# One product for two in the MLP's up-projection of a split-precision transformer block, with edits at the kernel's start and end

## The chip, the core and the metric

The kernel runs on one core of one Trainium2 chip. The metric is the device time of one execution in microseconds. The time of the kernel before is 2253.19 us, the median of three runs (2246.54 to 2254.56 us).

## What is computed

Two transformer blocks on 256 tokens of width 2048, all in float32. The first block mixes the tokens with a gated delta rule and an RWKV recurrence, attends to 256 memory tokens and ends with an MLP; the second has two kinds of local attention and a layer norm over each token. The part that the change is mostly about is the MLP, and the end of the program is the layer norm:

```python
hn = _rmsnorm(h, norm_mlp[l])                       # 256 x 2048
h = h + jnp.square(jax.nn.relu(hn @ mlp_w_up[l])) @ mlp_w_down[l]   # 2048 x 8192, 8192 x 2048
...
x = _layer_norm(DEEPNORM_ALPHA * x + out, ln_gain[layer], ln_bias[layer])
```

## The kernel before

**Split numbers.** Every large product is made of three. A float32 operand is split in a high part (rounded by ScalarE to the type that TensorE reads fast) and a low part (VectorE subtracts the high part from the number). Of weights W and activations x the kernel adds `hi(W) x hi(x)`, `hi(W) x lo(x)` and `lo(W) x hi(x)` in PSUM. For weights this is done in `piece` (L129 to L142): SyncE loads 256 rows and 512 columns (tile `raw`, 512 KB), `act` at L140 writes `whi`, the subtraction at L141 writes `wlo`. `raw`, `whi` and `wlo` have three buffers each. For activations `split` (L232) does it; the tiles are `ah` and `al`, each of 4 k-tiles of 128 rows and 256 tokens (`act_tiles`, L222, eight buffers in all).

**Two shapes of product.** `ws_parts` (L262) keeps the weights stationary: for each of four blocks `c` of 128 columns and each k-tile it gives TensorE three products with 256 tokens as the moving operand. The sums of two blocks share a PSUM bank (a bank holds 512 float32 columns), so four blocks take two banks. `as_parts` (L286) keeps the activations stationary and moves 512 columns of the weights, again three products for each k-tile and each half `t` of the tokens; `tail` says how many of the last pieces are held back, so that half 0 ends that much before half 1. `mm` (L100) issues all of these, so they all have line L101 in the profile, and `tt`, `stt` and `act` give VectorE's and ScalarE's instructions the lines L107, L116 and L104.

**The MLP** (L1229 to L1275). `mlp_up(b)` computes 2048 of the 8192 inner channels in four calls of `ws` (16 calls in all, 64 blocks of 128 channels, 16 k-tiles each), and `emit` (L1241) turns the sums of each block into its output: ScalarE's Relu from PSUM, VectorE's product of the sums with that, then `split` into `uh` and `ul`. `mlp_down(b)` uses `as_` and adds into `accd`. The order is up(0), up(1), down(0), up(2), down(1), up(3), down(2), down(3). `psum_phase(n)` (L85) divides the 8 PSUM banks: n for tiles of `mmt` (the sums), the rest for `pst`; from L1110 on there are four of each. Ahead of the MLP stand `xattn_wo` (L1218, `as_`) with the transposes of L1219; behind it `rstd` (L1278) and the second block.

**The order of the work.** Each engine has one queue, served in order. The program's order on each queue is laid down at build time by a scheduler that goes by priorities and its own times; only some stretches are ordered by hand (`manual_schedule`: TensorE in the first stage and in the last call of `as_`, SyncE's queue at the start).

**The start** (L151 to L173, L322 to L330): x and the first weights are loaded, x is transposed on TensorE (`tr`, L186) and split, and the 304 small columns of the first projection are computed from them (`ws` at L411).

**The end** (L1452 to L1479). The last product is added to `h`, VectorE takes the statistics, and `layer_norm(t)` normalises half `t` in four parts of 512 columns. Parts 0 to 2 of half 0 and part 0 of half 1 go over ScalarE (scale and shift), then a product with the gain and a sum with the bias, on GpSimd for half 0 (the third part's product on VectorE) and on VectorE for half 1; the other parts take two VectorE instructions each. Every part's output is issued on SyncE's queue.

```python
    for n in range(4):
        s = slice(512 * n, 512 * n + 512)
        if n < 3 - 2 * t:
            act(h[t][:, s], h[t][:, s], AF.Identity, scale=rl, bias=nb_)
```

Of the kernel before, what the change touches and what calls it, by code (L numbers as in the profile page):

```python
# [9 lines left out]
F32 = mybir.dt.float32  # L10
# [10 lines left out]
C_DECAY = 0.5 * math.exp(-0.5)  # L21
INV_LAT = 42.0
PART = 0.66

# [39 lines left out]
def block_kernel(tc, a, out, dbg=None, stop=99):  # L64
# [63 lines left out]

    def piece(W, r0, nk, cols, o=0):  # L129


        n = sum(c[1] for c in cols)
        with tc.high_priority():
            raw = fix.tile([128, nk, n], F32, name="raw", tag="raw", bufs=3)
            for c0, m, d in cols:
                nc.sync.dma_start(out=raw[:, :, d:d + m],
                                  in_=W[r0:r0 + nk * 128, c0:c0 + m].rearrange("(k p) n -> p k n", p=128))
            hi, lo = (fix.tile([128, nk * n + 64], F32R, name=x, tag=x, bufs=3)[:, o:o + nk * n]
                      .rearrange("p (k n) -> p k n", k=nk) for x in ("whi", "wlo"))
            last["act"] = act(hi, raw)  # L140
            last["dve"] = nc.vector.tensor_tensor(out=lo, in0=raw, in1=hi.bitcast(F32), op=SUB)  # L141
        return hi, lo  # L142
# [39 lines left out]
    xinit = cst[:, K_X0:K_X0 + 256]  # L182

    def tr(o, i):
        n = i.shape[0]
        nc.tensor.transpose(o, i, ident[0:n, 0:n])  # L186
# [34 lines left out]

    def act_tiles(where=None, bufs=8):  # L222

        hs, ls = [], []
        for _ in range(bufs // 2):
            h = (where or fix).tile([128, 4, T], F32R, name="ah", tag="act", bufs=bufs)
            l = (where or fix).tile([128, 4, T], F32R, name="al", tag="act", bufs=bufs)
            hs += [h[:, i, :] for i in range(4)]
            ls += [l[:, i, :] for i in range(4)]
        return hs, ls  # L230
# [31 lines left out]
    def ws_parts(W, cols, xh, xl, emit, kts=None, r0=0, needs=(), first=()):  # L262
# [19 lines left out]
        with tc.high_priority():  # L282
            for c in range(n):
                emit(c, acc[c // 2][:, c % 2, :])

    def as_parts(W, c0, xh, xl, emit, kts=None, r0=0, ahead=None, needs=(), tail=1):  # L286
# [682 lines left out]
    def main():  # L969
# [4 lines left out]
        def mem_in(i):  # L974

            q = i // 4
            if i >= 4:
# [3 lines left out]
                if i % 4 == 0:  # L981
                    ht, lt = (fix.tile([128, 4, T], F32R, name=n, tag="act", bufs=8) for n in ("ah", "al"))
                    for n, t_ in (("h", ht), ("l", lt)):
                        mem[n] += [t_[:, k, :] for k in range(4)]
                    with tc.high_priority():
                        rstd_part(lambda t, _: src[:, t, :], mem["ss"], q - 1)
# [228 lines left out]

    hh, hl = act_tiles()
    for n in range(4):
# [9 lines left out]


    rp2 = rstd(by_tok(h), "rmlp")  # L1229
    r2 = fix.tile([128, 2], F32, name="r2")  # L1230
# [4 lines left out]
    def mlp_up(b):  # L1235
        uh, ul = [], []
        for q in range(4):
            u1 = mp.tile([128, 4, T], F32R, name="uh", tag="u", bufs=16)
            u2 = mp.tile([128, 4, T], F32R, name="ul", tag="u", bufs=16)

            def emit(c, p, u1=u1, u2=u2):  # L1241
                r = mp.tile([128, T], F32, name="relu", tag="relu", bufs=2)
                act(r, p, AF.Relu)
                tt(r, p, r, MUL)
                split(r, u1[:, c, :], u2[:, c, :])
            ws(a["mlp_w_up"][0], [(2048 * b + 512 * q, 512, 0)], hh, hl, emit)
            uh += [u1[:, i, :] for i in range(4)]
            ul += [u2[:, i, :] for i in range(4)]
# [4 lines left out]
    def mlp_down(b, u):  # L1253
        for n in range(4):
# [10 lines left out]
            if b == 3:  # L1265
                transposed(by_tok(h), gains["final"], fh, fl, range(4 * n, 4 * n + 4))

# [8 lines left out]


    rf = rstd(by_tok(h), "rf")  # L1278
    sp2, close_s2 = open_pool("blk2")
# [149 lines left out]
    yp, close_y = open_pool("y")  # L1429
    shift(yp, 128)  # L1430
    for more, x in zip(act_tiles(yp, 4), (yh, yl)):
# [19 lines left out]

    def layer_norm(t):  # L1452
        mv = s2([128, 2], "mv", bufs=2)
        nc.vector.bn_aggr(out=mv, in_=st[t])
        rl = s2([128, 1], "rl", bufs=2)
        ts(rl, mv[:, 1:2], 1e-5, ADD)
        powc(rl, rl, mhalf[:, 0:1])
        nb_ = s2([128, 1], "nb_", bufs=2)
        stt(nb_, mv[:, 0:1], -1.0, rl, MUL, MUL)
        for n in range(4):  # L1460
            s = slice(512 * n, 512 * n + 512)
            if n < 3 - 2 * t:
                act(h[t][:, s], h[t][:, s], AF.Identity, scale=rl, bias=nb_)
                tt(h[t][:, s], h[t][:, s], lng[:, s], MUL, eng=nc.gpsimd if t == 0 and n < 2 else None)
                tt(h[t][:, s], h[t][:, s], lnb[:, s], ADD, eng=nc.gpsimd if t == 0 else None)
            else:
                stt(h[t][:, s], h[t][:, s], mv[:, 0:1], lng[:, s], SUB, MUL)
                stt(h[t][:, s], h[t][:, s], rl, lnb[:, s], MUL, ADD)
            nc.sync.dma_start(out=out[0, t * 128:(t + 1) * 128, s], in_=h[t][:, s])

    for n in range(4):
# [6 lines left out]
        with tc.manual_schedule(engines={nc.tensor.engine}) if n == 3 else nullcontext():  # L1478
            as_(a["w_out_2"][0], 512 * n, yh, yl, emit_o, tail=2 if n == 3 else 1)  # L1479
    close_ln()  # L1480
# [28 lines left out]
```

## Time and profile before

| | us |
|---|---|
| three runs, median (lowest to highest) | 2253.19 (2246.54 to 2254.56) |
| the profiled execution | 2262.2 |
| its span, first to last instruction | 2260.5 |
| busy in the span: TensorE products / its weight loads | 2200.2 / 2019.2 |
| VectorE / ScalarE / GpSimd | 1389.2 / 1120.5 / 269.4 |
| mean granted clock of TensorE | 0.986 |

The profile is of one execution; times in it count from the first instruction. TensorE's products overlap, so the time of one product (its row says 0.28 us) is longer than the distance from one start to the next, which is what counts in a dense stretch.

### The profile page before, as it was taken

The numbers are of one execution on the slowest core, as the hardware profiler recorded it, in microseconds if no ns is written. First come the engines' busy times: TensorE is split into PE (matmuls) and PEld (weight loads), VectorE is DVE, ScalarE is ACT, GpSimd is POOL, SyncE is SP. The second block draws the span as 40 slices with busy tenths as digits, with TensorE's granted clock in tenths as the row PEclk, the third lists the DMA queues.
The fourth block names the chain that finished last, engine by engine and source line by source line (L and its number), as shares of the span: only waits on it lengthen the run. The fifth ranks groups of instructions, "written<-read, shape, count | busy, mean of one in ns | idle before, by whom it ended". The sixth has DMA issues, their size and how long they took to land.

```text
span 2260.5 us, 39043 instructions
## 1 busy us (share of the span) xinstructions
PE 2200.2 (97%) x15506; PEld 2019.2 (89%) x15506; DVE 1389.2 (61%) x2236; ACT 1120.5 (50%) x1802; POOL 269.4 (12%) x540
## 2 busy tenths in 40 slices
PE   8999999999999999999999999999999999999996
PEld 8998989788988899889998898899888999888975
DVE  5576676675644555555554455555556676767765
ACT  5455554564444445445454444344344665656542
POOL 0027254165200000000000000000000000011101
PEclk9999999899999999999999999999999999999998
DMA  6654344353466654566666666666656667665654
GB/s 203 186 163 132 96 145 136 97 152 108 148 217 212 188 170 148 157 187 187 188 188 192 194 190 188 195 188 192 192 188 212 192 189 192 179 181 163 176 187 137
DMA packets 229061, 391.77 MB, mean 173 GB/s; under 512 B 39887, under 2 KB 47821, under 8 KB 228494
## 3 DMA queue, kind: packets, MB, share of 16 engines
q1 hardware_dynamic: 227297, 385.63, 56.8%
q10 hardware_dynamic: 1036, 3.58, 0.4%
q8 instruction: 121, 1.98, 0.3%
q14 instruction: 63, 0.51, 0.1%
q0 software_dynamic: 544, 0.07, 0.0%
HBM read 386.25 MB, written 2.97 MB: 172 GB/s over the span
## 4 chain that ended last, share of the span: by engine, by line
PE 87%; DVE 4%; DMA 3%; POOL 3%; ACT 2%; issue 1%; SPq 0%; POOLq 0%; ACTq 0%; DVEq 0%
PE acc L101 79%; POOL Xt L107 1%; DMA raw<-in_w_in_dram 1%; POOL X L107 1%; DVE wlo L141 1%; PE o2p L101 1%; PE s2p L101 1%; DMA nb<-scr 1%; PE t2p L186 1%; PE op L101 1%; PE xs L101 0%; PE xo L101 0%; ACT whi L104 0%; PE tp L186 0%; DMA rT<-in_mem_dram 0%
## 5 line engine op out<-in xcount | busy, mean ns | idle before, releaser
L141 DVE TENSOR_TENSOR wlo<-raw,whi 128x1024 fp32r<-128x1024 f32 (+1 forms) x696 | 853.3, 1227 | 697.7 <-ACT whi L104 692.8
L104 ACT ACTIVATE whi<-raw 128x1024 fp32r<-128x1024 f32 (+1 forms) x696 | 734.9, 1057 | 854.3 <-PE acc L101 734.4
L101 PE MATMUL acc<-ah,whi 128*128 128x256 f32 x3120 | 885.6, 284 | 2.5 <-DVE ey L107 1.8
L101 PE MATMUL acc<-al,whi 128*128 128x256 f32 x3120 | 876.2, 281 | 0.0
L101 PE MATMUL acc<-ah,wlo 128*128 128x256 f32 x3120 | 873.1, 281 | 1.3 <-DVE wlo L141 1.3
L101 PEld LDWEIGHTS acc<-ah,whi 128*128 128x128 f32 x3120 | 589.6, 189 | 8.5 <-issue 3.1
L101 PEld LDWEIGHTS acc<-al,whi 128*128 128x128 f32 x3120 | 589.9, 189 | 1.4 <-issue 0.9
L101 PEld LDWEIGHTS acc<-ah,wlo 128*128 128x128 f32 x3120 | 588.1, 189 | 2.6 <-DVE wlo L141 2.4
L101 PE MATMUL acc<-whi,al 128*128 128x512 f32 x704 | 275.8, 392 | 0.0
L101 PE MATMUL acc<-wlo,ah 128*128 128x512 f32 x704 | 275.7, 392 | 0.0
L101 PE MATMUL acc<-whi,ah 128*128 128x512 f32 x704 | 265.4, 397 | 4.0 <-DVE qky L107 2.6
L101 PE MATMUL acc<-wlo,uh 128*128 128x512 f32 x512 | 199.5, 390 | 0.0
L101 PE MATMUL acc<-whi,ul 128*128 128x512 f32 x512 | 199.2, 389 | 0.0
L101 PE MATMUL acc<-whi,uh 128*128 128x512 f32 x512 | 179.5, 389 | 0.0
L101 PEld LDWEIGHTS acc<-whi,ah 128*128 128x128 f32 x704 | 132.9, 189 | 30.8 <-DVE qky L107 2.8
L101 PEld LDWEIGHTS acc<-whi,al 128*128 128x128 f32 x704 | 133.1, 189 | 27.8
L101 PEld LDWEIGHTS acc<-wlo,ah 128*128 128x128 f32 x704 | 133.3, 189 | 26.6
L101 PEld LDWEIGHTS acc<-whi,ul 128*128 128x128 f32 x512 | 96.1, 188 | 20.0
L101 PEld LDWEIGHTS acc<-whi,uh 128*128 128x128 f32 x512 | 96.1, 188 | 19.8
L101 PEld LDWEIGHTS acc<-wlo,uh 128*128 128x128 f32 x512 | 96.1, 188 | 19.7
L107 POOL TENSOR_TENSOR Xt<-X,nb 128x60 f32<-128x60 f32 (+24 forms) x186 | 80.1, 431 | 162.4 <-DMA nb<-scr 148.6
L1351 POOL MEMSET klz<- 64x256 f32 x8 | 2.5, 307 | 701.5 <-DMA raw<-in_w_in_dram 701.2
(523 smaller groups left out, 1869.3 us busy)
## 6 DMA issues: line engine op xcount, KB each, us to landing
raw<-in_w_in_dram SPq DMA_DIRECT2D x240, 512.0 KB, 3.7
raw<-in_mlp_w_up_dram SPq DMA_DIRECT2D x128, 512.0 KB, 3.7
raw<-in_mlp_w_down_dram SPq DMA_DIRECT2D x128, 512.0 KB, 3.9
raw<-in_w_out_dram SPq DMA_DIRECT2D x64, 512.0 KB, 4.7
raw<-in_xattn_wk_dram SPq DMA_DIRECT2D x32, 512.0 KB, 3.9
raw<-in_xattn_wv_dram SPq DMA_DIRECT2D x32, 512.0 KB, 5.4
raw<-in_xattn_wq_dram SPq DMA_DIRECT2D x32, 512.0 KB, 3.8
raw<-in_xattn_wo_dram SPq DMA_DIRECT2D x32, 512.0 KB, 3.9
```

The costliest lines, as they stand in the source:

```text
L101: nc.tensor.matmul(o, l, r, start=start, stop=stop)
L104: return nc.scalar.activation(o, i, f, **kw)
L107: (eng or nc.vector).tensor_tensor(out=o, in0=x, in1=y, op=op)
L141: last["dve"] = nc.vector.tensor_tensor(out=lo, in0=raw, in1=hi.bitcast(F32), op=SUB)
L186: nc.tensor.transpose(o, i, ident[0:n, 0:n])
L1351: nc.gpsimd.memset(kl[other, e, :].bitcast(F32), 0.0)
```

## The change

- `ws_both` replaces `ws` in `mlp_up`: `hi(W)` meets `hi(x)` and `lo(x)` in one product of 512 columns (the moving operand is two runs of 256 columns, 1024 elements apart), and `lo(W)` meets `hi(x)` in one of 256, which goes to the first half of the bank. Each block of 128 channels has a bank of its own, and `emit` adds the two halves first: one copy on ScalarE and one sum on VectorE more for each block.
- For that, the high and low parts of four k-tiles of x lie in one tile (`act_tiles`, and the same tiles in the first stage); the tag has four buffers of twice the size. The `wlo` tile of `ws_both` is used from element 56 on, the `whi` tile from 0.
- PSUM is divided 7 and 1 for the MLP, and 4 and 4 again behind it; the transposes of the last down-projection take their tiles from the seven.
- Start: eleven products of 512 columns on a tile of zeros, ahead of the rest, into a tile that nothing reads.
- End: all parts but one go over VectorE alone; the last part of half 1 goes over ScalarE and GpSimd and is issued on ScalarE's queue; `tail` is 3, not 2. One placement constant is 160, not 128.

```diff
+WARM = 11
-    def piece(W, r0, nk, cols, o=0):
+    def piece(W, r0, nk, cols, o=0, ol=None):
...
+    idle = xnp.tile([128, 512], F32R, name="idle")
+    nc.vector.memset(idle.bitcast(F32), 0.0)
+    with tc.high_priority():
+        spare = mmt([128, 512], "spare")
+        for i in range(WARM):
+            mm(spare, idle[:, 0:128], idle, start=(i == 0), stop=(i == WARM - 1))
...
-            h = (where or fix).tile([128, 4, T], F32R, name="ah", tag="act", bufs=bufs)
-            l = (where or fix).tile([128, 4, T], F32R, name="al", tag="act", bufs=bufs)
-            hs += [h[:, i, :] for i in range(4)]
-            ls += [l[:, i, :] for i in range(4)]
+            x = (where or fix).tile([128, 2, 4, T], F32R, name="ah", tag="act", bufs=bufs // 2)
+            hs += [x[:, 0, i, :] for i in range(4)]
+            ls += [x[:, 1, i, :] for i in range(4)]
+            if both is not None:
+                both += [x[:, :, i, :] for i in range(4)]
...
+    def ws_both(W, c0, xh, xb, emit):
+        acc = [mmt([128, 2, T], "acc") for _ in range(4)]
+        for i in range(0, 16, 2):
+            hi, lo = piece(W, i * 128, 2, [(c0, 512, 0)], 0, 56)
+            for c in range(4):
+                cc = slice(c * 128, c * 128 + 128)
+                for j in range(2):
+                    k = i + j
+                    mm(acc[c], hi[:, j, cc], xb[k], start=(k == 0), stop=False)
+                    mm(acc[c][:, 0, :], lo[:, j, cc], xh[k], start=False, stop=(k == 15))
+        with tc.high_priority():
+            for c in range(4):
+                emit(c, acc[c])
...
+    psum_phase(7)
     rp2 = rstd(by_tok(h), "rmlp")
...
             def emit(c, p, u1=u1, u2=u2):
                 r = mp.tile([128, T], F32, name="relu", tag="relu", bufs=2)
-                act(r, p, AF.Relu)
-                tt(r, p, r, MUL)
+                y = mp.tile([128, T], F32, name="up", tag="up", bufs=2)
+                act(y, p[:, 1, :])
+                tt(y, p[:, 0, :], y, ADD)
+                act(r, y, AF.Relu)
+                tt(r, y, r, MUL)
                 split(r, u1[:, c, :], u2[:, c, :])
-            ws(a["mlp_w_up"][0], [(2048 * b + 512 * q, 512, 0)], hh, hl, emit)
+            ws_both(a["mlp_w_up"][0], 2048 * b + 512 * q, hh, hb, emit)
...
+    psum_phase(4)
     rf = rstd(by_tok(h), "rf")
...
-    shift(yp, 128)
+    shift(yp, 160)
...
+        own = cols[0:4 - t]
+        def centre(s):
+            stt(h[t][:, s], h[t][:, s], mv[:, 0:1], lng[:, s], SUB, MUL)
+        def finish(s):
+            stt(h[t][:, s], h[t][:, s], rl, lnb[:, s], MUL, ADD)
             nc.sync.dma_start(out=out[0, t * 128:(t + 1) * 128, s], in_=h[t][:, s])
+        for s in own[0:2]:
+            centre(s)
+        if t == 1:
+            s = cols[3]
+            nb_ = s2([128, 1], "nb_")
+            stt(nb_, mv[:, 0:1], -1.0, rl, MUL, MUL)
+            act(h[t][:, s], h[t][:, s], AF.Identity, scale=rl, bias=nb_)
+            tt(h[t][:, s], h[t][:, s], lng[:, s], MUL, eng=nc.gpsimd)
+            tt(h[t][:, s], h[t][:, s], lnb[:, s], ADD, eng=nc.gpsimd)
+        for s in own[0:2]:
+            finish(s)
+        for s in own[2:]:
+            centre(s)
+            finish(s)
+        if t == 1:
+            s = cols[3]
+            nc.scalar.dma_start(out=out[0, t * 128:(t + 1) * 128, s], in_=h[t][:, s])
...
-            as_(a["w_out_2"][0], 512 * n, yh, yl, emit_o, tail=2 if n == 3 else 1)
+            as_(a["w_out_2"][0], 512 * n, yh, yl, emit_o, tail=3 if n == 3 else 1)
```

## Rows read from the trace of the kernel before

**Rows 1.** The page's busy table: busy us, share of the span, instructions.

```profile
PE 2200.2 (97%) x15506; PEld 2019.2 (89%) x15506; DVE 1389.2 (61%) x2236; ACT 1120.5 (50%) x1802; POOL 269.4 (12%) x540
```

**Rows 2.** Windows in the MLP: length, busy us by engine, clock, DMA share, GB/s.

```profile
1060.00:1130.00 70.00, 70.00 (x602) 70.00 (x602) 39.01 (x50) 34.17 (x51) 0.00 (x0) 1.00 0.65 189
1600.00:1727.00 127.00, 127.00 (x575) 105.45 (x574) 71.31 (x76) 56.60 (x71) 2.46 (x8) 1.00 0.60 190
```

**Rows 3.** Waits of 1020 to 1740 us: total, times, longest.

```profile
ACT whi L104 <- PE acc L101: 349.1, 232, 1.8
...
PEld acc L101 <- DVE wlo L141: 0.2, 1, 0.2
```

**Rows 4.** Chain that ended last, in order of time: products of 256, then of 512 columns.

```profile
55.87 54.24 PE acc L101 x464
...
1665.66 21.78 PE acc L101 x96
```

**Rows 5.** The tile relu: count, then shortest, median, longest ns.

```profile
L104 ACT ACTIVATE relu<-acc x64: 362/366/388, 1038.6 to 1556.8; 128x256 f32<-128x256 f32 x64
L107 DVE TENSOR_TENSOR relu<-acc,relu x64: 416/418/420, 1039.3 to 1558.1; 128x256 f32<-128x256 f32 x64
```

**Rows 6.** Timeline of ScalarE, then of VectorE, behind one call of ws.

```profile
1038.56 0.39 ACT L104 ACTIVATE relu<-acc 128x256 f32<-128x256 f32 x1 [0.45 <-PE acc L101]
...
1060.96 0.39 ACT L104 ACTIVATE relu<-acc 128x256 f32<-128x256 f32 x1 [0.45 <-PE acc L101]
...
1040.94 1.22 DVE L141 TENSOR_TENSOR wlo<-raw,whi 128x1024 fp32r<-128x1024 f32 x1 [1.24 <-ACT whi L104]
1042.09 0.42 DVE L107 TENSOR_TENSOR ul<-relu,uh 128x256 fp32r<-128x256 f32 x1
1042.42 0.42 DVE L107 TENSOR_TENSOR relu<-acc,relu 128x256 f32<-128x256 f32 x1
1043.79 1.23 DVE L141 TENSOR_TENSOR wlo<-raw,whi 128x1024 fp32r<-128x1024 f32 x1 [0.95 <-ACT whi L104]
```

**Rows 7.** Timeline of VectorE behind the last down-projection.

```profile
1726.40 1.28 DVE L107 TENSOR_TENSOR accd<-acc,accd 128x512 f32<-128x512 f32 x2
```

**Rows 8.** Timeline of the start: first transposes and first products.

```profile
6.01 4.34 PE L186 MATMUL tp<-cst,xn 128*128 128x128 f32 x18
...
9.48 0.71 ACT L104 ACTIVATE whi<-raw 128x608 fp32r<-128x608 f32 x1
...
10.62 0.41 PE L101 MATMUL acc<-al,whi 128*128 128x256 f32 x1
...
11.26 0.41 PE L101 MATMUL acc<-ah,wlo 128*128 128x256 f32 x1
```

**Rows 9.** Timeline of TensorE, then the window 36 to 38 us.

```profile
35.63 0.41 PE L101 MATMUL acc<-ah,whi 128*128 128x256 f32 x1
...
38.83 0.29 PE L101 MATMUL acc<-ah,whi 128*128 128x256 f32 x1
...
36.00:38.00 2.00, 2.00 (x12) 2.00 (x11) 1.69 (x5) 0.38 (x1) 0.00 (x0) 0.50 0.86 259
```

**Rows 10.** Timeline of VectorE at the end.

```profile
2239.68 0.69 DVE L116 SCALAR_TENSOR_TENSOR h<-h,acc 128x512 f32<-128x512 f32 x1 [3.12 <-PE acc L101]
...
2241.49 0.74 DVE L116 SCALAR_TENSOR_TENSOR h<-h,mv,lng 128x512 f32<-128x512 f32 x1
...
2245.12 2.41 DVE L116 SCALAR_TENSOR_TENSOR h<-h,mv,lng 128x512 f32<-128x512 f32 x2
...
2254.71 0.69 DVE L107 TENSOR_TENSOR h<-h,lnb 128x512 f32<-128x512 f32 x1
```

**Rows 11.** Timeline of GpSimd, then of ScalarE, at the end.

```profile
2243.78 3.21 POOL L107 TENSOR_TENSOR h<-h,lng 128x512 f32<-128x512 f32 x2 [1.12 <-ACT h L104]
2246.94 1.71 POOL L107 TENSOR_TENSOR h<-h,lnb 128x512 f32<-128x512 f32 x1
...
2251.03 0.81 ACT L104 ACTIVATE h<-h,nb__23786,rl 128x512 f32<-128x512 f32 x1 [5.92 <-DVE nb__23786 L116]
```

More of the change, by code (lines that the diff above doesn't have):

```diff
@@ L137, in piece @@
                                   in_=W[r0:r0 + nk * 128, c0:c0 + m].rearrange("(k p) n -> p k n", p=128))
-            hi, lo = (fix.tile([128, nk * n + 64], F32R, name=x, tag=x, bufs=3)[:, o:o + nk * n]
-                      .rearrange("p (k n) -> p k n", k=nk) for x in ("whi", "wlo"))
+            hi, lo = (fix.tile([128, nk * n + 64], F32R, name=x, tag=x, bufs=3)[:, b:b + nk * n]
+                      .rearrange("p (k n) -> p k n", k=nk) for x, b in (("whi", o), ("wlo", o if ol is None else ol)))
             last["act"] = act(hi, raw)
@@ L220, in row_bcast, with act_tiles @@
         return o
-    def act_tiles(where=None, bufs=8):
+    def act_tiles(where=None, bufs=8, both=None):
         hs, ls = [], []
         for _ in range(bufs // 2):
-            h = (where or fix).tile([128, 4, T], F32R, name="ah", tag="act", bufs=bufs)
-            l = (where or fix).tile([128, 4, T], F32R, name="al", tag="act", bufs=bufs)
-            hs += [h[:, i, :] for i in range(4)]
-            ls += [l[:, i, :] for i in range(4)]
+            x = (where or fix).tile([128, 2, 4, T], F32R, name="ah", tag="act", bufs=bufs // 2)
[3 more added lines that the diff above has]
+                both += [x[:, :, i, :] for i in range(4)]
         return hs, ls
@@ L981, in mem_in @@
                 if i % 4 == 0:
-                    ht, lt = (fix.tile([128, 4, T], F32R, name=n, tag="act", bufs=8) for n in ("ah", "al"))
+                    x = fix.tile([128, 2, 4, T], F32R, name="ah", tag="act", bufs=4)
+                    ht, lt = x[:, 0], x[:, 1]
                     for n, t_ in (("h", ht), ("l", lt)):
@@ L1214, in block_kernel @@
     close_km()
-    hh, hl = act_tiles()
+    hb = []
+    hh, hl = act_tiles(both=hb)
     for n in range(4):
@@ L1265, in mlp_down @@
             if b == 3:
-                transposed(by_tok(h), gains["final"], fh, fl, range(4 * n, 4 * n + 4))
+                transposed(by_tok(h), gains["final"], fh, fl, range(4 * n, 4 * n + 4), mmt)
     u = mlp_up(0)
@@ L1452, in layer_norm @@
     def layer_norm(t):
+        cols = [slice(512 * n, 512 * n + 512) for n in range(4)]
         mv = s2([128, 2], "mv", bufs=2)
@@ L1457, in layer_norm @@
         powc(rl, rl, mhalf[:, 0:1])
[L1458 to L1468, printed above, removed]
-            nc.sync.dma_start(out=out[0, t * 128:(t + 1) * 128, s], in_=h[t][:, s])
+        own = cols[0:4 - t]
[3 more added lines that the diff above has]
+            stt(h[t][:, s], h[t][:, s], rl, lnb[:, s], MUL, ADD)
+            nc.sync.dma_start(out=out[0, t * 128:(t + 1) * 128, s], in_=h[t][:, s])
+        for s in own[0:2]:
[15 more added lines that the diff above has]
+            nc.scalar.dma_start(out=out[0, t * 128:(t + 1) * 128, s], in_=h[t][:, s])
     for n in range(4):
```

## The prediction, made before the changed kernel ran

> **What bounds the kernel now.** I read the busy table first, then the windows of the MLP, its waits, the chain of waits for the distance of products, and last the timelines of both ends. In the busy table TensorE has 97% of the span [rows 1], so only time taken out of its queue counts, or time at the ends, where it has nothing to do. In the MLP this is exact: it is busy for 70.00 of 70.00 us in the up-projection and 127.00 of 127.00 in the down-projection, at full granted clock [rows 2]. Its weight loads wait 0.2 us in 720 us for a low part of the weights, and ScalarE waits 349.1 us for TensorE to free a buffer [rows 3]. So weights are ready before they are needed; the DMA, with 189 GB/s at a share of 0.65 [rows 2], is not the limit either. A change here is worth what it does to the sum of the distances between products.
>
> **The MLP's products.** In the chain of waits 464 products of 256 columns take 54.24 us, 116.9 ns each, and 96 of 512 take 21.78 us, 226.9 ns each [rows 4]. Two of 256 are 233.8 ns: the long one saves 6.9 ns, about what one instruction costs beyond its columns. For each block and k-tile, three products (350.7 ns) become one of 512 and one of 256 (343.8 ns). There are 16 calls x 4 blocks x 16 k-tiles = 1024 of these: **-7.1 us**. A call goes from 22.40 us, the distance between the two first Relus of two calls [rows 6], to 64 x 343.8 ns = 22.0 us. A third of the products goes, but hardly any column, and columns are what TensorE's time is made of.
>
> No row has a 512-column product in the reduced type whose moving operand is two runs 1024 elements apart. From above I bound it by two products of 256, 233.8 ns (then nothing is gained). From below: in the cold stretch 256 columns take 0.213 us at a granted clock of 0.50, that is 1.2 GHz [rows 9], one column each cycle; at 2.4 GHz 512 columns are then 213.3 ns, and the gain is 20.5 ns x 1024 = 21 us. I take 226.9, the row of the same length and type. The offset of the low parts only moves addresses, and I cost it at nothing within these bounds.
>
> The Trainium skill, "TensorE: Matmul & The Clock Gate", section "Back-to-back issue gap", speaks against the change: it gives a warm gap of N / 2.4 plus 2.5 ns, which leaves 2.5 ns for each product saved, 2.6 us in all and 2248.9 us for the sum below. The measured distances disagree: 116.9 ns stands 10.2 over 256 / 2.4.
>
> **What emission adds.** Each of 64 blocks gets a copy on ScalarE (as the Relu from PSUM, 366 ns) and a sum on VectorE (418 ns) more [rows 5]: 23.4 and 26.8 us of work. I cost both at nothing, since VectorE is busy for 39.0 and ScalarE for 34.2 us of 70 [rows 2]. TensorE's products cover them; without that cover some 27 us would be on the path. Two waits could take the cover away. First, a bank: a call takes 4 of 7, so its fourth block needs the bank of the call before's first block. That block's sums end 3 blocks (2.06 us) ahead of its call's end, and the bank is asked for 2.06 us into the next call. Copy and sum (0.37 + 0.42 us), even behind one wlo of 1.22 us [rows 6] and a high part of about the same, fit into 4.1 us. Second, the weights: a high part starts when its buffer is freed and its low part must be there two pieces later, 5.5 us; two instructions of at most about 1.2 us leave some 3 us. In today's timeline two emission instructions stand between two wlo's [rows 6], and three would add 0.42 us. So nothing.
>
> **Divided PSUM.** The first call needs four banks at once where two did, while the last output-projection still holds two; behind the MLP the banks change hands again. The nearest row is the pair of sums that frees two such banks, 1.28 us [rows 7]: 0 to 1.3 us at each border. I take 0.25 each, since the next banks are mostly free: **+0.5 us**. The merged tiles of x are freed as pairs; both parts of a k-tile are last read in the same piece, so this is nothing.
>
> **Start.** The first transposes stand at 6.01 us, and the first products after 10.24 us lie 0.213 us apart from 10.62 to 11.26 [rows 8], as in the stretch at a clock of 0.50 [rows 9]. Eleven products of 512 columns at 1.2 GHz are 11 x 0.427 = 4.7 us; started with the program, they end about when the transposes start. If the clock then is up at 10.6 us, five products save 0.096 us each, 0.5 us. Before that the high part of the weights, at 9.48 us, waits for its DMA, which no warm engine hastens. The second slow stretch, 35.63 to 38.83 us with 15 products [rows 9], follows a gap of its own and stays: 15 x 0.096 = 1.4 us that may go if the phase shifts. I take **-0.4 us**, between +0.4 (the zeros delay the transposes) and -1.9.
>
> **End.** Half 0 now ends 18 products ahead of half 1, not 12: VectorE starts 6 x 0.227 = 1.36 us earlier, at 2238.32 instead of 2239.68 [rows 10]. From there to the first centring it takes 1.81 us, and a part's instruction 0.74 [rows 10]. Half 0 has eight of these: 1.81 + 5.92 = 7.73 us, until 2246.05. Half 1 has 1.81 + 6 x 0.74 = 6.25 us: 2252.3. Its last part leaves VectorE after two centrings, at about 2249.4; ScalarE takes 0.81, GpSimd 1.6 and 1.7 [rows 11], so 2253.5. Beside GpSimd two VectorE instructions took 2.41 us instead of 1.48 [rows 10, 11], so VectorE ends at 2253.2 rather. Today it ends at 2254.71 + 0.69 = 2255.40 [rows 10]. The output's DMA behind that I leave as it is: SyncE's queue no longer has a part of GpSimd's in front of finished ones, and nothing stands behind the one on ScalarE's. **-1.8 us**, between -3.1 (no mutual waiting) and -0.9 (twice as much).
>
> **Sum.** -7.1 + 0.5 - 0.4 - 1.8 = -8.8 us. The profiled execution would go from 2262.2 to 2253.4; it lies 9.0 us above the median. From the median, 2253.2 - 8.8 = **2244.4 us**, 0.4% less. A measurement of this kernel tells about 0.5%, 11.3 us, from no change, and its three runs lie 8 us apart.
>
> **Rivals.**
> - *Two runs cost as two products.* The chip would gain nothing from one instruction with a gap in its operand, the change not doing what it says: 2253.2 - 1.7 = 2251.5. For it: no row shows the shape. Against: 256 columns in a run are long beside the 6.9 ns at stake. 0.12.
> - *The long product nears one column a cycle.* If its 13.6 ns beyond the columns halve, at 220 ns, 13.8 ns are gained each time, 14.1 us: 2237.4. For it: a fixed weight tile meets twice the columns. Against: the 512-column rows of both projections have 226.9. 0.12.
> - *The saved cost is a smaller one.* Of the 6.9 ns half belongs to the instruction, the rest to how the operands of the two shapes lie: 3.5 us are gained in place of 7.1, 2248.0. Against: each shape keeps its distance in other stages [rows 4]. 0.06. By the Trainium skill's gap, as above, it would be 2248.9.
> - *Slower: emission holds up the weights.* If the scheduler puts the 12 VectorE instructions of a call's emission (12 x 0.42 = 5.0 us) between two wlo's, the slack of about 3.2 us is passed by 1.8 us in each of 16 calls: +29 us, 2273. It decides from eight instructions in a row; two stand there now [rows 6]. VectorE's work in a call, by 39.0 of 70 us plus 4 x 0.42, remains under two thirds. 0.07.
>
> **Chances.** The forecast has the other 0.63. Its bounds (MLP's half steps, ends, borders) and the scatter of runs and an order laid anew by the scheduler put about a third of it under 2241.9, which is 0.5% off; with the second rival 0.33 for faster. Over 2264.5 only the last rival lies: 0.07. The rest, 0.60, is within 0.5%. The range 2237 to 2255 takes in the first three rivals and the bounds of the small terms, and leaves out the last rival and the far end of the second.
>
> **What would show it.** In the changed profile a product of 512 columns with whi stationary should be followed at 226.9 ns by one of 256 that takes 116.9, and the first emission instructions of two calls should be 22.0 us apart. TensorE stays gapless in the MLP, with VectorE at some 63% there. The products behind 10 us stand 0.117 us apart, and VectorE's last instruction ends about 1.8 us nearer to the last product. The forecast is wrong if the long product is not within 220 to 231 ns, or if TensorE waits for wlo or for emission at the ends of calls.

## The result, and the profile after

| | before | after |
|---|---|---|
| median (lowest to highest), 6 runs each on one chip, us | 2253.97 (2246.54 to 2255.86) | 2266.67 (2263.45 to 2272.69) |
| ratio, 95% interval | | 1.0052 [1.0037, 1.0066] |
| profiled execution / its span, us | 2262.2 / 2260.5 | 2267.18 / 2265.5 |
| third run of 96 products ahead of the MLP to the first scores of block 2 (**A**) | 803.23 | 817.74 |
| from there to the start of the last run of products (**B**) | 376.46 | 371.69 |
| from there to the end of the span (**C**) | 103.85 | 99.52 |

The change makes the kernel 12.7 us slower where 8.8 us faster was forecast. A, B and C are read off the chain of waits, which has these starts. Before:

```profile
976.96 21.78 PE acc L101 x96
...
1780.19 2.29 PE acc L101 x10
...
2156.65 83.00 PE acc L101 x354
```

After:

```profile
976.55 21.78 PE acc L102 x96
...
1794.29 2.31 PE acc L102 x10
...
2165.98 80.85 PE acc L102 x348
```

The MLP lies in A and loses 14.5 us; the second block and the end win back 9.1. The 970 us ahead of A can't be compared between two profiles: the recurrent stage in it took 543 to 559 us in the profiles of this study, whatever the kernel.

The busy table and two windows of the changed kernel, columns as in [rows 1] and [rows 2]:

```profile
PE 2201.5 (97%) x14493; PEld 1972.1 (87%) x14493; DVE 1408.9 (62%) x2303; ACT 1138.8 (50%) x1863; POOL 265.0 (12%) x537
...
1060.00:1130.00 70.00, 70.00 (x400) 60.95 (x398) 42.28 (x62) 38.05 (x62) 0.00 (x0) 1.00 0.64 187
...
1655.00:1745.00 90.00, 82.92 (x387) 68.27 (x386) 50.59 (x62) 41.32 (x62) 3.15 (x9) 0.98 0.56 183
```

The kernel before, in the last of these windows:

```profile
1655.00:1745.00 90.00, 89.69 (x481) 77.23 (x480) 58.63 (x69) 44.59 (x64) 3.17 (x9) 1.00 0.63 197
```

A thousand products are gone, and TensorE is as busy as before. In the up-projection it is gapless; in the last down-projection [rows 2] and behind it, it misses 7.1 us of 90, where the kernel before misses 0.3.

**The calls.** TensorE's timeline inside a call:

```profile
1077.66 0.40 PE L102 MATMUL acc<-ah,whi 128*128 128x512 f32 x1
1077.90 0.28 PE L102 MATMUL acc<-ah,wlo 128*128 128x256 f32 x1
1078.01 0.39 PE L102 MATMUL acc<-ah,whi 128*128 128x512 f32 x1
1078.24 0.28 PE L102 MATMUL acc<-ah,wlo 128*128 128x256 f32 x1
1078.36 0.39 PE L102 MATMUL acc<-ah,whi 128*128 128x512 f32 x1
```

A pair takes 0.35 us. Over all calls but the first the start of a short product lies 232.8 ns behind that of the long one before it, the next long one 119.3 to 119.7 ns behind the short one: 352 ns where 343.8 was taken and where three products took 350. Eight times a call the scheduler lays two long products in a row; in thirteen of these fifteen calls the second then starts 234 ns behind the first, no less than a short one would. ScalarE's timeline has the first copies of two calls 22.53 us apart, where [rows 6] has 22.40:

```profile
1039.64 0.37 ACT L105 ACTIVATE up<-acc 128x256 f32<-128x256 f32 x1
...
1062.17 0.37 ACT L105 ACTIVATE up<-acc 128x256 f32<-128x256 f32 x1
```

**The transposes of the last down-projection.** TensorE's timeline, then the chain of waits:

```profile
1661.88 0.39 PE L102 MATMUL acc<-wlo,uh 128*128 128x512 f32 x1
1662.11 0.39 PE L102 MATMUL acc<-whi,ul 128*128 128x512 f32 x1
1664.05 0.66 PE L195 MATMUL tp<-cst,h 128*128 128x128 f32 x4 [1.55 <-DVE h L117]
1664.46 0.48 PE L102 MATMUL acc<-whi,uh 128*128 128x512 f32 x1
```

```profile
1659.81 1.07 ACT whi L105
...
1660.91 1.23 DVE wlo L142
1662.13 1.20 DVE accd L108 x2
1663.33 0.67 DVE h L117
1664.00 0.04 issue
1664.05 0.66 PE tp L195 x4
```

The first transposes stand right behind the last product of their sum, and wait until VectorE is done with a low part, with the sums and with `h`: 1.94 us from the last product's start, at 1662.11, 1686.57, 1711.03 and 1735.50. Before, with `pst` tiles, 26 products stood between them (the fourth time 35 short ones), and `h` was done 3.6 us before the transposes came up. In the timeline of the kernel before, the sum's last product, `h` and the transposes:

```profile
1658.50 0.39 PE L101 MATMUL acc<-whi,ul 128*128 128x512 f32 x1
...
1659.64 1.40 DVE L116 SCALAR_TENSOR_TENSOR h<-accd,r,h 128x512 f32<-128x512 f32 x2
...
1664.62 1.03 PE L186 MATMUL tp<-cst,h 128*128 128x128 f32 x8
```

**The MLP's entry**, TensorE's timeline. The transposes ahead of it now wait for VectorE, and the third sum needs a bank whose transposes VectorE hasn't split yet:

```profile
1015.84 0.39 PE L102 MATMUL acc<-whi,ah 128*128 128x512 f32 x1
1016.52 1.25 PE L195 MATMUL tp<-cst,h 128*128 128x128 f32 x8 [0.29 <-DVE h L108]
...
1018.19 0.28 PE L102 MATMUL acc<-ah,wlo 128*128 128x256 f32 x1
1019.42 0.50 PE L102 MATMUL acc<-ah,whi 128*128 128x512 f32 x1 [0.95 <-DVE ah L117]
```

The 14.5 us of A are then: 2.0 in the calls (16 x 0.127), 1.9 at the entry, 5.5 in the last two down-projections (182.01 us from their start to the last sum's product, before 176.56; three of the waits lie in it) and 5.1 behind it, the fourth of the waits and a slow stretch after it among them.

### The profile page after: what moved, and what is told of

The parts are those of the page before. It is cut to its first block, busy times and chain, and to the rows that moved or that the text cites. A ratio compares the mean times of both kernels' runs of the same rounds, so it can differ in the third digit from the quotient of the medians.

```text
span 2265.5 us, 37154 instructions
## 1 busy us (share of the span) xinstructions
PE 2201.5 (97%) x14493; PEld 1972.1 (87%) x14493; DVE 1408.9 (62%) x2303; ACT 1138.8 (50%) x1863; POOL 265.0 (12%) x537
## 4 chain that ended last, share of the span: by engine, by line
PE 83%; POOL 6%; DVE 4%; DMA 2%; ACT 2%; issue 2%; SPq 0%; POOLq 0%; ACTq 0%; DVEq 0%
PE acc L102 76%; POOL Xt L108 2%; POOL X L108 2%; DVE wlo L142 1%; DMA nb<-scr 1%; DMA raw<-in_w_in_dram 1%; PE s2p L102 1%; PE o2p L102 1%; ACT whi L105 1%; PE t2p L195 1%; PE xs L102 0%; PE xo L102 0%; PE op L102 0%; PE tp L195 0%; DVE gv L117 0%
## 5 line engine op out<-in xcount | busy, mean ns | idle before, releaser
L102 PE MATMUL acc<-ah,whi 128*128 128x256 f32 (+2 forms) x5216 | 1121.5, 306 | 5.3 <-ACT ah L105 2.0
L102 PEld LDWEIGHTS acc<-ah,whi 128*128 128x128 f32 (+1 forms) x5216 | 836.5, 189 | 51.8 <-issue 3.8
L102 PE MATMUL acc<-ah,wlo 128*128 128x256 f32 x3120 | 857.0, 281 | 2.6 <-DVE wlo L142 2.6
L102 PE MATMUL acc<-whi,ah 128*128 128x512 f32 x1408 | 446.5, 393 | 4.0 <-DVE qky L108 2.6
L102 PEld LDWEIGHTS acc<-whi,ah 128*128 128x128 f32 x1408 | 264.3, 188 | 58.2 <-DVE qky L108 2.8
L108 POOL TENSOR_TENSOR X<-X,Xt 128x60 f32<-128x60 f32 (+24 forms) x186 | 75.5, 406 | 14.1
L108 POOL TENSOR_TENSOR bias<-bias,namask 128x256 f32<-128x256 f32 x32 | 30.1, 944 | 363.8 <-DVE s L114 235.7
L105 ACT ACTIVATE ah<-tp,par 128x256 fp32r<-128x256 f32 x80 | 32.7, 475 | 12.8 <-PE tp L195 9.4
L105 ACT ACTIVATE s<-s,mx 128x256 f32<-128x256 f32 x64 | 31.9, 499 | 10.7 <-DVE mx L112 10.5
```

The lines of the kernel that those rows point to most:

```text
L102: nc.tensor.matmul(o, l, r, start=start, stop=stop)
L105: return nc.scalar.activation(o, i, f, **kw)
L108: (eng or nc.vector).tensor_tensor(out=o, in0=x, in1=y, op=op)
```

## The experiments

In the order in which they ran. A ratio is to the kernel before, timed beside it; where none stands, the kernel was profiled once and not compared in time. A, B and C are those of the table.

**1. One run of 512 columns.** The long product's operand without a gap.

```diff
-            x = (where or fix).tile([128, 2, 4, T], F32R, name="ah", ...)
...
-                both += [x[:, :, i, :] for i in range(4)]
+            x = (where or fix).tile([128, 4, 2, T], F32R, name="ah", ...)
...
+                both += [x[:, i, :, :] for i in range(4)]
```

> The high and low parts of a k-tile now lie side by side, so the moving operand of the long product is one run of 512 elements; the rest is the changed kernel. Theory (an operand in two runs costs 235.3 ns, as two products, not 226.9): the distance between the first emission copies of two calls falls from 22.53 us to 22.0 us, and the time by 16 x 0.53 = 8.5 us, to about 2258 us, ratio to the kernel before about 1.002. Rival (the 8.4 ns come from something else in the new pattern: the bank for each block, the offset of the low parts, the change between lengths): 22.53 us and 2266 us, as in the changed kernel.

Measured: 1.0052 [1.0040, 1.0064], a call still 22.53 us, A 817.31. The two runs of the operand are not the cause.

**2. The transposes back in their own banks.**

```diff
-                transposed(..., range(4 * n, 4 * n + 4), mmt)
+                transposed(..., range(4 * n, 4 * n + 4))
...
+            psum_phase(4)        # ahead of down(3)
...
-    psum_phase(4)                # behind the MLP
```

> PSUM is divided 4 and 4 already ahead of the last down-projection, and its transposes take their tiles from the small share as before; the rest is the changed kernel. Theory (from the share of the sums, the transposes are queued directly behind the product whose result they need, and TensorE waits four times for VectorE, about 2 us each, the last time with a slow stretch behind it): TensorE's four waits for h are gone, the stretch from the first section of the last down-projection to the second block is 10 to 12 us shorter, the time about 2256 us, ratio 1.001. Rival (the time is lost by handing the banks over, wherever that stands): the loss moves ahead of the last down-projection and the time stays at 2264 to 2268 us.

Measured: 1.0010 [0.9998, 1.0023], A 807.99, 9.8 us less. In the chain eight transposes stand together again, and nothing waits ahead of them. So the tag that the transposes share with the sums is the greater part of the loss. The entry's 1.9 us stay.

**3. Everything but the MLP.** The changed kernel with the MLP of before (`ws`, the old `emit`, no new PSUM division).

> The up-projection, the emission and the division of PSUM are those of the kernel before; the edits at the start and the end, the merged tiles and the placement stay. Theory (the end gains about 3.5 us, and the start's 3.6 us are lost again before 750 us to waits of the recurrent stage): 2248 to 2251 us, ratio about 0.998. Rival (the ends, or the merged tiles, cost part of the 12.7 us): 2256 us or more, ratio over 1.001.

Measured: 0.9988 [0.9973, 1.0003]; A 803.86 as before, B 371.99, C 99.41. The whole loss of A comes with the new MLP and its transposes; the shorter B and C come without it.

**4. Experiments 1 and 2 together.**

> e1 and e2 together. Theory (two separate losses): the gains add, 8.5 and about 11 us from 2266.7, to about 2247 us, ratio 0.997. Rival (one loss hides behind the other, or the order laid by the scheduler decides): less than two thirds of the sum of the two, 2254 us or more.

Measured: 1.0003 [0.9993, 1.0012], A 808.33: nothing beyond experiment 2.

**5. Sixteen places of the weights.** Each call of the changed kernel with another pair of offsets (0 to 64 elements) for `whi` and `wlo`, and the tiles of x shifted by 0 to 48 elements.

> e1 with other places for the operands: each of the 16 calls uses its own pair of offsets for the high and the low parts of the weights (0 to 64 elements), and the four tiles of x start 0, 16, 32 and 48 elements in. Rival 1 (addresses: two operands that lie badly to each other cost the long product its 8 ns): calls, or the quarters of a call, differ by 0.1 us and more, the best reaches 22.0 us for a call. Rival 2 (the shape: activations move past weights, and each column costs what it did): all calls stay within 22.45 to 22.60 us, whatever the offsets.

Measured: calls of 22.30 to 22.47 us, none near 22.0. From start to start a pair costs 348.4 to 351.6 ns, 350.1 in the mean of the fifteen calls behind the first, where experiment 1 has 352.0. The place moves the price by up to 1%, but no place tried here reaches the forecast.

**6. The kernel before, profiled again.**

> The kernel before, unchanged, for a second profile. If the changed kernel's 5 to 9 us between the first scores of the second block and the end are the change's, this profile shows some 480 us there as the first did (480.31 us); if they are scatter of that stage, some 474 us, only 4 us over the changed kernel's 471. Its stage ahead of the MLP scatters by several us whatever the kernel.

Measured: A 804.06, B 375.02, C 103.88. What the first profile showed is typical. The gain in C belongs to the change; that in B is less sure, since experiment 11 has 372.76 without the merged tiles and experiment 2 has 374.64 with them.

**7. The new end alone** (`layer_norm` and `tail=3`, filler of 128 bytes).

> The kernel before with the new layer norm and tail 3 alone. Theory: the last stretch is 4.3 us shorter, ratio 0.998, some 2251.5 us against 2256. Rival (the gain is the new placement's or the start's): under 2 us, ratio 0.999 or more.

Measured: 0.9992 [0.9979, 1.0005], so no gain in time that is clear of noise; C 101.86, 2.0 us less.

**8. The products on zeros alone** (`WARM`).

> The kernel before with the eleven products on zeros alone. Theory (gained at the start, lost in the recurrent stage, which waits for its own chain of GpSimd and DMA): the long run of 464 products starts 2 to 4 us earlier than at 55.87 us, and the time stays within 1.5 us of before, ratio 0.9993 to 1.0007. Rival (what is gained at the start stays gained): 2 to 4 us less, ratio 0.998 to 0.999.

Measured: 1.0007 [0.9992, 1.0023]. The run of 464 products begins at 53.12 us; in two profiles of the kernel before it begins at 55.87 and 53.69. No gain that can be told.

**9. The filler alone**, `shift(yp, 160)` in the kernel before.

> The kernel before with one number changed: the filler ahead of the tiles of y is 160 bytes and not 128. Nothing is added to or taken from any engine. Theory (operand addresses set the price of a product): the last run of 348 products falls from 83.1 us to about 80.7 us, the 375 us of block 2 ahead of it (which don't use these tiles) stay as they are, and the ratio is about 0.999. Rival (the gain in the last run came from the merged tiles of the operands): the last run stays at 83.1 us, and the ratio is 1.000.

Measured: 1.0000 [0.9989, 1.0012]; C 105.05, and the last run 84.23 us, longer and not shorter. TensorE's timeline of the kernel before, then of this one, one low part's product to a later one:

```profile
2206.38 0.39 PE L101 MATMUL acc<-wlo,ah 128*128 128x512 f32 x1
...
2207.29 0.39 PE L101 MATMUL acc<-wlo,ah 128*128 128x512 f32 x1
```

```profile
2206.59 0.40 PE L101 MATMUL acc<-wlo,ah 128*128 128x512 f32 x1
...
2208.45 0.40 PE L101 MATMUL acc<-wlo,ah 128*128 128x512 f32 x1
```

The first stretch is 4 products of 227.5 ns, the second 8 of 232.5. Over 54 us of the run, from 28 to 82 us behind its start, the distances are 226 or 227 ns before, and up to 235 here, 230.2 in the mean. The filler changes nothing but addresses: the same products cost 1.5% more in another place. Experiment 7 has 230.2 too, the changed kernel and experiment 11 have 226.7.

**10. The merged tiles alone.**

> The kernel before with the high and low parts of x in one tile of 2 x 4 x 256 and not in two of 4 x 256; the MLP, both ends and the filler of 128 bytes as before. Theory: the merged tiles are what makes block 2 ahead of its last section shorter by 2 to 3.5 us (they change the addresses of all operands and when the buffers come free), and cost nothing ahead of 747 us: ratio about 0.9985. Rival: two buffers that come free together hold up the loads and splits ahead of 747 us by 2 to 4 us, which takes the gain back: ratio 1.000 or a little above.

Measured: 0.9999 [0.9986, 1.0013]; A 803.94, B 372.52, C 102.89. The chain of this kernel ahead of 747 us, and of the kernel before at the same place:

```profile
604.64 0.44 PE ot L186 x4
605.08 9.00 PE acc L101 x77
...
614.13 1.24 DVE wlo L141
```

```profile
609.41 0.44 PE ot L186 x4
609.85 14.24 PE acc L101 x122
```

Here the rival finds part of its wait. VectorE splits nine of sixteen tiles of `mix` before the weights' low part is let in, where it split four; TensorE waits 1.3 us for it. From these transposes to the next run of 96 products it is 139.43 us, before 138.02, and the changed kernel (139.42) and experiment 2 have the wait too. The tiles' B is 2.5 to 3.9 us shorter, as the theory has it, though B falls as low in a kernel without them (11); in the time nothing is left of it.

**11. The new end and the filler**, no more.

```diff
-    shift(yp, 128)
+    shift(yp, 160)      # with layer_norm and tail=3 of the changed kernel
```

> The kernel before with the new end (layer norm and the tail of three) and the filler of 160 bytes; MLP, tiles and start as before. Theory: the end's 2.0 us and the last run's 2.3 us add up: last section 99.5 us where it was 103.9, ratio about 0.998. Rival: no gain from the filler: last section 101.9 us, ratio about 0.999.

Measured: **0.9974 [0.9964, 0.9984]**, 2250.11 us: the lowest time and ratio of the study, below both kernels. C is 100.43, 1.4 less than with the end alone, and the products of the last run are back at 226.7 ns: the filler undoes what the end's own tiles do to the addresses. B is 372.76, 3.7 us less than in the first profile, though nothing in it was changed. 1.6 us of that is one fall of the clock that doesn't come; the rest isn't accounted for. The windows of the kernel before, then of this one, over the same products:

```profile
2012.00:2014.00 2.00, 2.00 (x6) 1.54 (x6) 0.52 (x1) 1.06 (x1) 1.43 (x2) 0.50 0.18 44
```

```profile
2004.30:2006.30 2.00, 2.00 (x11) 1.64 (x10) 0.71 (x1) 1.50 (x2) 1.47 (x2) 1.00 0.17 41
```

Both came out of a wait of 2.6 us; one ran at 1.2 GHz, the other at 2.4.

**12. Weights loaded once a call.** One of eight pieces is loaded and split and used for all eight.

> The changed kernel, with one of the eight pieces of a call's weights loaded and split (the first) and used for all eight: 7 of 8 loads, high-part copies and low-part subtractions of the MLP's first product are left out, and its output is of other weights; the products, their number, shapes and operand tiles of x stay. A look at why the long product costs 232 to 235 ns and not 227. Theory (loads, copies and subtractions that write to the on-chip memory while TensorE reads its operands slow the reading): behind the first piece of a call the pair of products falls from 352 ns to 325 to 340 ns, a call from 22.52 to some 21 to 22 us, and sixteen calls give back 8 to 24 us. Rival (the price belongs to the products themselves, 0.457 ns a column whatever goes on beside them): the pair stays at 350 to 352 ns and a call at 22.4 to 22.6 us.

Measured: a call still 22.59 us, 0.06 more than in the changed kernel. The window of a call, changed kernel and this one:

```profile
1062.40:1084.90 22.50, 22.50 (x129) 19.62 (x128) 13.80 (x21) 12.25 (x21) 0.00 (x0) 1.00 0.63 187
```

```profile
1062.40:1084.90 22.50, 22.50 (x129) 19.57 (x129) 5.60 (x14) 5.14 (x14) 0.00 (x0) 1.00 0.08 24
```

With the DMA's share down from 0.63 to 0.08 and VectorE's work more than halved, TensorE takes as long. The traffic beside it is not the cause.

**13. Other operands in the long product.**

`v` is the number of the call in its block, 0 to 3.

```diff
+                    fixed = xh[k][:, 0:128] if v == 2 else hi[:, j, cc]
+                    moved = hi[:, j, :] if v == 1 else xb[0] if v == 3 else xb[k]
-                    mm(acc[c], hi[:, j, cc], xb[k], ...)
+                    mm(acc[c], fixed, moved, ...)
```

> The changed kernel, with another operand in the long product of three of a block's four calls of the MLP's first product: call 0 as it is (weights' high part held, x moving); call 1 moves the weights' high part, 512 columns in a row, through the same held block; call 2 holds 128 columns of x's high part and moves x; call 3 holds the weights and moves the same k-tile of x (the first) in all sixteen. The output is another one in calls 1 to 3; number and shapes of the products stay. Theory A (the price goes with the moving operand: x at 0.457 ns a column, weights at the 0.443 of the second product): call 1 falls from 22.52 us to 22.0 to 22.1, calls 0, 2 and 3 stay at 22.4 to 22.55. Theory B (it goes with the held operand: a held block of weights costs more than one of x): call 2 falls to 22.0 to 22.1, call 1 stays. Theory C (neither: it goes with the sequence of a long and a short product, or with where the sums are written): all four stay at 22.4 to 22.55 us.

Measured: 233 ns behind the long product and 119 to 120 behind the short one in all four kinds of call. Theories A and B fall; exchanging either operand leaves the price. Of theory C only the sequence is tried below (14); where the sums are written, four banks in turn and the short product in the first half of its bank, was never varied and stays a rival.

**14. Grouped.** The same products, eight long ones and then eight short ones of each piece.

```diff
-            for c in range(4):
-                ...
-                    mm(acc[c], hi[:, j, cc], xb[k], ...)
-                    mm(acc[c][:, 0, :], lo[:, j, cc], xh[k], ...)
+            kc = [(i + j, j, c, slice(c * 128, c * 128 + 128)) for c in range(4) for j in range(2)]
+            for k, j, c, cc in kc:
+                mm(acc[c], hi[:, j, cc], xb[k], ...)
+            for k, j, c, cc in kc:
+                mm(acc[c][:, 0, :], lo[:, j, cc], xh[k], ...)
```

> The changed kernel, with the same products in another order: of each piece of weights first the eight long products (512 columns), then the eight short ones (256), where the changed kernel alternates long and short. Nothing else differs. In runs of one length a product of 512 columns measures 226 to 227 ns and one of 256 columns 116 to 117; alternating, 233 and 119.7. Theory (changing the length from product to product costs some 9 ns a pair): a call falls from 22.52 us to about 22.0 (64 x 343.5 ns, and two changes a piece left), sixteen calls give back 7 to 9 us, ratio about 1.0015. Rival (the price is of this stage, whatever the order): the call stays at 22.4 to 22.55 us, ratio 1.005.

Measured: 1.0034 [1.0021, 1.0048], A 814.15, 3.6 us less. TensorE's timeline:

```profile
1070.78 1.99 PE L102 MATMUL acc<-ah,whi 128*128 128x512 f32 x8
1072.61 1.09 PE L102 MATMUL acc<-ah,wlo 128*128 128x256 f32 x8
1073.54 2.01 PE L102 MATMUL acc<-ah,whi 128*128 128x512 f32 x8
```

This piece takes 2.76 us, the mean is 2.78, eight of them 22.24, where alternating it is 22.53 and the forecast 22.0. With the operands where they lie here, the order is about half of the miss: a pair falls from 352.0 to 347.3 ns. Within a group a long product still takes 230 ns.

**15. Grouped, and the transposes in their own banks.**

> The order of products of the run before this one, and in it the last down-projection's transposes back in their own small banks, as in the run that did that alone (ratio 1.001, four waits of 1.9 us gone). Theory (both costs are real and add up): the stretch from the start of the last cross-attention products before the MLP to the first scores of block 2, 817.7 us in the changed kernel and 803.2 before, falls to about 800, and the ratio is about 0.997 to 0.998. Rival (the order of the products gives nothing): 808 us and 1.001.

Measured: 0.9990 [0.9975, 1.0004], A 803.15. The two repairs add up (14.6 us), and the new MLP then costs just what the old one does: the calls' gain, 16 x 0.18 = 2.8 us, goes at the borders (2.4 at the entry, 0.4 behind the MLP).

**16. The same with one run of 512 columns.**

> The run before this one (grouped products, transposes in small banks), and in it x's high and low part of a k-tile side by side, so that the long product's operand is one run of 512 columns. Grouped, a long product behind a long one measures 230 ns with two runs of 256, where the second product's, with one run, measures 226 to 227, and the call 22.2 us. Theory (what grouping left over is the two runs, which the alternation had covered): long products at 226 to 227 ns, a call at 21.95 to 22.05 us, sixteen calls 3 us less, ratio about 0.997 to 0.998. Rival (what is left goes with addresses and not with the run's shape): 229 to 231 ns, calls 22.15 to 22.3, ratio 0.999.

Measured: 0.9986 [0.9974, 0.9997]; 230.1 ns for a long product and A 803.63. The rival holds: the shape of the operand is not what is left.

**17. Grouped, the weights in sixteen places.**

> The grouped products (transposes in small banks), and in each of the sixteen calls another place of the weights in their tiles: the high parts start at element 0, 4, 8, ... 60, the low parts at 60 less that. A look only: distances of long products within a group, call by call. Theory (what grouping left over, 230 ns against 226 to 227, is the place of the operands, as in the last projection, where the same products measure 226.7 ns with the filler of before and 230.2 with it alone changed): some offsets give 226 to 227 ns and others 230 or more. Rival (the price is of this stage, whatever the place): 229 to 231 at every offset.

Measured: long products of 229.4 to 234.3 ns within a group, call by call, short ones of 114 to 119. TensorE's timeline at offset 0, then at offset 24:

```profile
1024.22 2.00 PE L102 MATMUL acc<-ah,whi 128*128 128x512 f32 x8
1026.06 1.10 PE L102 MATMUL acc<-ah,wlo 128*128 128x256 f32 x8
1026.99 2.00 PE L102 MATMUL acc<-ah,whi 128*128 128x512 f32 x8
```

```profile
1164.33 2.04 PE L102 MATMUL acc<-ah,whi 128*128 128x512 f32 x8
1166.20 1.12 PE L102 MATMUL acc<-ah,wlo 128*128 128x256 f32 x8
1167.16 2.04 PE L102 MATMUL acc<-ah,whi 128*128 128x512 f32 x8
```

A piece costs 2.77 or 2.83 us by the place alone; but no offset gives 226.7, so each theory has half of it. What the remaining 3 ns a product (some 4 us in all) hang on is open.

This run also limits experiment 14. Over the fifteen calls behind the first a pair costs 345.0 to 352.9 ns here, 350.3 in the mean: grouped products cost as much, over these places, as alternating ones over those of experiment 5 (350.1). High parts that start 4 elements further, at the same place of the low parts, already take the grouped pair from 347.3 (14) to 350.2. So the order is shown to be worth 4.7 ns at one place. That it is worth anything at another isn't shown; no other place was run in both orders.

## Why the prediction was wrong, point by point

- **What bounds the kernel**: right for the kernel before, and for the up-projection still: experiment 12 takes most of VectorE's work and of the DMA away, and a call takes as long. But "a change here is worth what it does to the sum of the distances between products" holds only while TensorE's queue stays gapless, and the moved transposes put four waits into it.
- **The MLP's products, -7.1 us**: +2.0 measured. The step that failed here is "the long one saves 6.9 ns" (a second one, the transposes, follows below): both prices came from stages where every product has one length. Here the long product takes 232.8 ns, outside the 220 to 231 ns that the prediction set as its own test, and the short one 119.5; at about 0.46 ns a column an instruction less saves nothing. The value lay inside the bounds that the prediction itself gave, 213.3 to 233.8, and nearer to the upper end than to the row it chose. The rival "two runs cost as two products" had the size of this term nearly right and the reason wrong (experiments 1 and 16). What the runs show in its place: order and place of the operands together move a pair between 345.0 and 352.9 ns (5, 14, 17), and no run reaches 343.8. How the two share it is open, and about 4 us stay unexplained in any case.
- The Trainium skill, "TensorE: Matmul & The Clock Gate", section "Back-to-back issue gap", gives N / 2.4 plus 2.5 ns for an isolated warm product, an estimate of 325 ns for the pair. No call measured here has a pair under 345.0; that dropping an instruction is worth little agrees with the 352 against 350 measured.
- **Emission, nothing**: right, and so the slower rival fell. VectorE is at 42.28 us of 70, 60% where some 63% was forecast. Slower came another way.
- **Divided PSUM, +0.5 us**: 1.9 at the entry (2.4 where the products are grouped, 15), and with both repairs 0.4 behind the MLP. "The next banks are mostly free" was wrong: the third sum had to wait for VectorE to split the transposes in its bank.
- **The transposes in the sums' tag, not costed**: about 9.8 us by experiment 2, the largest single loss. The diff shows the edit; the prediction treated it as part of the division and never asked what stands in front of a moved instruction on TensorE's queue. In the old order 26 products, 5.9 us, hid VectorE's sums, `h` and one low part; now nothing does, and 1.94 us pass from the sum's last product to the transposes, four times. This is the second step that failed, a term put at nothing without a reason, and the larger one.
- **Low part's offset and filler, nothing**: places are worth 1 to 2% of the products that they touch (5, 9, 17), and two edits that each cost that much undo each other (7, 9, 11). The bounds allowed for it; the sum did not.
- **Merged tiles, nothing**: they change the order that the scheduler lays. 1.4 us are lost at the mix (10), some 2.5 to 3.9 gained in block 2, part of that a clock fall that comes or not, and not clear of what block 2 does unchanged (11).
- **Start, -0.4 us**: nothing measurable (8).
- **End, -1.8 us**: -2.0 measured (7), but that agreement is luck. It contains products at 230 ns in the last run; with these back at 226.7 C is 3.4 us shorter (11), beyond the forecast's -3.1. The part that was argued came true: before, the last engine's work ends 98.75 us behind the run's start [rows 10], in experiment 11 at 96.80, 1.95 earlier. GpSimd's timeline there:

```profile
2241.08 1.59 POOL L107 TENSOR_TENSOR h<-h,lnb 128x512 f32<-128x512 f32 x1
```

The other 1.5 us lie behind it, in the output's DMA, which the prediction left as it was: from the last work to the end of the span it is 5.1 us before and 3.6 here. The changed kernel's 99.52 is 0.9 less again, since the clock is back sooner in the last run. These windows, of the kernel before and after, start 4 and 2 us behind the run's start:

```profile
2160.65:2162.65 2.00, 2.00 (x8) 1.57 (x7) 2.00 (x4) 1.34 (x4) 0.00 (x0) 0.68 0.50 197
```

```profile
2167.98:2169.98 2.00, 2.00 (x7) 1.58 (x6) 1.90 (x6) 1.56 (x3) 0.00 (x0) 0.61 0.97 406
```

At 1.2 GHz the run spends its first 5.3 us before, its first 3.6 after.

The profiles' stretches add up to +14.5 - 4.8 - 4.3 + 1.4 = +6.8 us; the medians differ by 12.7. The same reckoning, each kernel's own median against its stretches from 747 us on and the wait at the mix, leaves 1.7 to 5.5 us over for the nine kernels with merged tiles that were timed, and -1.2 to +1.9 for the four without. So some 3 us more seem to go with the merged tiles ahead of 605 us, where the order of every engine's instructions is that of before. That is a pattern over thirteen kernels with one profile each, and not shown; the scatter of the recurrent stage hides where, and it stays open.

## What to carry to other kernels

Take a product's price from a stage with the same sequence of lengths and try it at more than one place of the operands: grouping by length saved 4.7 ns a pair at one place and nothing in the mean over the places tried. Saving instructions without saving columns is worth 2% of their time at best (343.5 ns for 350), which the place of the operands can take back. When a tile moves to another PSUM tag, its instructions move in TensorE's queue: list what the first of them waits for and which products stood in front of it before. Try an edit's parts alone: here the end with its filler (0.9974) was worth having, and the main part, even repaired, was not (A 803.15 against 803.23).

## What the runs showed of the hardware that was not expected

- Products of 512 columns in the reduced type, each with a new held block, lie 226 to 227 ns apart in the last projection, 230 there with a filler of 32 bytes more (9), and 233 when they alternate with products of 256, which themselves go from 116.7 to 119.5. In groups of eight they lie 229.4 to 234.3 apart, by the place of the weights (17).
- Neither which operand moves (13), nor the gap in it (1, 16), nor a DMA share of 0.63 or 0.08 beside it (12) changed the price of a pair by more than 1 ns in 352.
- Behind the same wait of 2.6 us the clock fell to 1.2 GHz for some eight products in one kernel and not in another with the same instructions around it (18 products in 5.99 or 4.38 us).
